# Moving the first loads into the order of use, fetching raw weight tiles ahead of their preparation, and keeping the value tiles for a whole head pair

## The chip, the cores and the metric

The kernel runs on one core of a Trainium2 chip. The core has a matrix engine (TensorE, PE in the rows; PEld is its weight load), a vector engine (VectorE, DVE), an activation engine (ScalarE, ACT), a general engine (GpSimd, POOL) and a queue engine (SyncE, SP) that here issues all transfers. Each engine runs its own list of instructions in order; they meet through semaphores. The metric is device time of one execution in microseconds (us), the median of three runs.

## The reference, cut to what matters

One layer over x of 2048 tokens by 1024 features: a normalised x is projected by one weight matrix, its columns feed three branches, and an output projection and a norm end it.

```python
h = rmsnorm(x, norm_g);  p = h @ w_in          # 1664 rwkv columns, 1544 fox, 1024 gate
# rwkv: token shift, then per head a recurrence over time
w = w0 + tanh(wl) @ w_up;  a = sigmoid(a0 + al @ a_up)
state = state*decay + sa (x) (kk*a) + v (x) k;  y = state @ r      # 8 heads of 64
# fox: causal attention with a decay from the cumulated log forget gate, 8 heads of 64
s = (q @ k.T) * scale + c_q - c_k;  o = softmax(mask(s)) @ v
y = concat(y_rwkv, y_fox) * silu(gate);  out = rmsnorm(x + y @ w_out, final_g)
```

## The kernel before, in words

Every product with `w_in` is made from halves: x and the weights are each split into a float16 high part and a float16 low part, and three matmuls (high by high, low by high, high by low) make one product. So a raw weight tile (128 columns, 512 KB of float32) has to be prepared before use: `prep_w` (L192) issues its load (L199), DVE takes its largest values (`am_`, L200, once per tile), PE turns them over the partitions (`px_`, L170 and L177), DVE works out a power of two per column group and scales the tile (L216), ACT copies the high half (L218) and POOL subtracts for the low half (L219). Raw tiles live in the three buffers of the tag `wr`; one is free again when POOL has made its low half.

**The first stage** (to about 1020 us) runs over four head pairs p and, in each, over four blocks b of 512 tokens. `load_x_block` (L138) loads four x tiles of a block, normalises and transposes them. At p = 0 each block also projects the low-rank columns (`pj_l`). Each (p, b) projects three weight tiles (`pj_r`, L254), shifts them, and runs `prep` (L471), a chain over DVE, ACT, POOL and PE that ends in the products `pb` and `pk` (L541, L544) and in stores (`d_ga`, `d_gl`, `d_ar`, `d_nk`, `d_vn`, `d_bo`). `inverse` (L574) inverts the triangular blocks of a finished pair, mostly on DVE, and `inverse_end` (L601) ends with the store `d_z` of the tile `z` (L619). Constants at L34 say at which b these happen: weights of the next pair at b = 2, inverse of the last pair at b = 1, its end at b = 2.

**Fillers.** `step(n)` draws n units from the generator `fillers` (L390): per unit one block of a fox projection (`fox_proj`, matmuls `pf`, L332) or half a gate column group (`gate_proj`). There are seven groups of three (once two) weight tiles; the weights of a group are prepared by `group_w` (L383) after the first unit of the group before. `fox_proj` also writes the value tiles `vh`, `vl` (L320 to L322, L346, L347) and stores them to `d_v`.

**Order.** The source gives the program's order; a scheduler then places each engine's instructions by its own timing model, so that the lists of all engines change when a piece of code moves. The engines follow the lists strictly: an instruction that waits holds all behind it on its engine. The later stages are attention with the rwkv chain in its gaps (about 1020 to 1460 us) and the output projection (to the end).

**Start.** Loads are issued in this order: `g_c`, four x tiles of block 0, the low-rank weight tile `wr_l`, `mu_c`, five columns of per-channel parameters (`w0_c` to `rk_c`, 2 KB each, 512 runs of one element), two of the three tiles of pair 0 (the third needs a `wr` buffer that `wr_l` holds), the forget columns `wf`, further parameter columns, `lup`, and then x blocks 1 to 3. In the rows `w_c` and `a_c` are `w0_c` and `a0_c`, `hw_c`, `ha_c`, `hka_c` and `oka_c` what DVE derives from these columns, `x`, `xt` the x tiles, `xp` their transposes, `hhi`, `hlo` the halves of x.

Of the kernel before, what the change touches and what calls it, by code (L numbers as in the profile page):

```python
# [39 lines left out]
def hymba_body(tc, x, norm_g, w_in, rw_mu, rw_w_up, rw_w0, rw_a_up, rw_a0, rw_k_k, rw_k_a, rw_r_k,  # L40
# [7 lines left out]
    with ctx:  # L48
# [32 lines left out]
        def pcol(src, n, name):  # L81
            t = ctile(name, [128, n])
            nc.sync.dma_start(t, src.rearrange("o (j p) -> p (o j)", p=128))
            return t
# [104 lines left out]
            ts(isc[:, 0:n].bitcast(I32), e, 23, ALU.logical_shift_left)  # L189
            return sc  # L190

        def prep_w(n, offs, tag, outs, iall):  # L192

            nt = len(offs)
            am = wp.tile([128, 3, KT, 2], F32, name="am_" + n, tag="am")
            wrs = []
            for i, c0 in enumerate(offs):
                wr = wp.tile([128, KT, 128], F32, name=f"wr_{n}{i}", tag="wr", bufs=3)
                nc.sync.dma_start(wr, w_in[0, :, c0:c0 + 128].rearrange("(k p) n -> p k n", p=128))  # L199
                nc.vector.tensor_reduce(am[:, i].rearrange("q k g -> q (k g)"),  # L200
                                        wr.rearrange("q k (g c) -> q (k g) c", c=64), AX.X, ALU.max,
                                        apply_absolute_value=True)
                wrs.append(wr)
# [17 lines left out]
        def load_tiles(name, offs):  # L221

            iall = wp.tile([128, 6], F32, name="ia_" + name, tag="ia", bufs=2)
            ws = [(wp.tile([128, KT, 128], F16, name=f"wh_{name}{i}", tag="wh", bufs=3),
                   wp.tile([128, KT, 128], F16, name=f"wl_{name}{i}", tag="wl", bufs=3)) for i in range(len(offs))]
            prep_w(name, offs, "r", ws, iall)
            return ws, iall

        def load_w(name, offs, extra=None):
# [4 lines left out]
            cs = [slice(128 * i, 128 * i + 128) for i in range(len(offs))]  # L234
            prep_w(name, offs, "f", [(wh[:, :, c], wl[:, :, c]) for c in cs], iall)
# [69 lines left out]
        def fox_proj(p, fw, w):  # L305
# [7 lines left out]
            nc.vector.tensor_copy(iq, isc[:, 0:4])  # L313
            i2 = F(f"i2{p}", "i2", (128, 4), bufs=2)
            nc.vector.scalar_tensor_tensor(i2, iq, 1.0 / HD, iq, ALU.mult, ALU.mult)
            for b in range(NB):
                u = f"{p}_{b}"
                t0 = b * TB
                hh, hl = hT[b]
                vh = F("vh" + u, "vh", (128, 2, 4, 66), F16)  # L320
                vl = F("vl" + u, "vl", (128, 2, 4, 64), F16)
                nc.gpsimd.memset(vh[:, :, :, 64:66], 1.0)  # L322
                qkt = [F(f"qkt{u}_{i}", f"qt{i}", (128, 2, TB), F16) for i in range(2)]
                qkn = []
# [86 lines left out]
        with c1:  # L411
# [224 lines left out]
            sml, sol = mix_scales("l", iscl, 1, mu_c[:, 12:13], omu_c[:, 12:13])  # L636

            def rw_weights(p):
                ws, isc = load_tiles(f"r{p}", [i * 512 + p * 128 for i in range(3)])
                sm, so = mix_scales(f"r{p}", isc, 3, mu_c[:, p:p + 9:4], omu_c[:, p:p + 9:4])  # L640
                return ws, sm, so

            rw = [rw_weights(0)]
# [15 lines left out]
            uh = sp.tile([128, 2, 512], F32R, name="uh")  # L659
            ul = sp.tile([128, 512], F32R, name="ul")  # L660
            up = T("lup", "rs")
            nc.sync.dma_start(up[0:64, :], rw_w_up[0])
            nc.sync.dma_start(up[64:128, :], rw_a_up[0])
            for i, (q0, q1) in enumerate(HR):
                for o0, o1 in HR:
                    nc.scalar.activation(uh[o0:o1, i], up[q0:q1], AF.Copy)
                nc.gpsimd.tensor_tensor(ul[q0:q1], up[q0:q1], uh[q0:q1, i].bitcast(F32), ALU.subtract)
            for b in range(1, NB):
                load_x_block(b, sp, ps_r)
# [488 lines left out]
```

## Time and profile before

| | us |
|---|---|
| median of three runs (1704.86, 1715.65, 1716.54) | 1715.65 |
| the profiled execution | 1709.08 |
| its span, first to last instruction | 1707.4 |
| mean granted TensorE clock, as a share of 2.4 GHz | 0.962 |

The page gives for each engine its busy time; rows of a time line give start, duration, engine, line, operation, what is written from what, and in brackets the idle time before and what ended it. Wait rows give who waited for whom, the sum, the number of waits and the longest. The profiled execution lies 6.6 us under the median.

### The profile page before, as it was taken

Reading aid. Unit: us, or ns where it says so; the run is one execution under the profiler, and the core shown is the slowest. Engines: PE = TensorE matmul, PEld = TensorE weight load, DVE = VectorE, ACT = ScalarE, POOL = GpSimd, SP = SyncE. Lnnn points to the kernel's source line nnn. Section 1 sums busy time; section 2 is a strip of 40 time slices with the busy share of each in tenths; the row PEclk is TensorE's granted clock in tenths of the full one; section 3 lists DMA queues with packets and bytes.
Section 4 is the critical chain, followed back from the end, with each engine's and each line's share of the span. In section 5 each row is a group of like instructions: output and inputs, shape, how many; then the busy total and the mean of one; then the engine's idle time right before and its main releaser. Section 6 shows DMA issues by size and latency. Waiting matters only on the chain. (4 is left out here: it accounts for less than half of the span.)

```text
span 1707.4 us, 36607 instructions
## 1 busy us (share of the span) xinstructions
PE 1575.2 (92%) x14182; PEld 974.5 (57%) x14182; DVE 1210.0 (71%) x2614; ACT 839.9 (49%) x1583; POOL 766.9 (45%) x838
## 2 busy tenths in 40 slices
PE   4899799899998999999999999899999998899998
PEld 2455355455544564445453566566666665567886
DVE  4866568975888669743844678588999997975443
ACT  5644444445433454445343247566776677564221
POOL 5754554545345543532201135455666666663000
PEclk9899899999998999999999999899999998899999
DMA  6432232233213242322234029666879633733452
GB/s 180 124 100 87 97 114 87 87 112 122 103 69 118 82 143 74 117 96 106 96 102 130 26 63 253 158 150 159 186 169 208 144 99 79 214 99 103 164 173 75
DMA packets 211983, 207.74 MB, mean 122 GB/s; under 512 B 53664, under 2 KB 173472, under 8 KB 211296
## 3 DMA queue, kind: packets, MB, share of 16 engines
q1 hardware_dynamic: 211808, 205.39, 42.1%
q8 instruction: 112, 1.84, 0.5%
q14 instruction: 63, 0.52, 0.1%
HBM read 123.34 MB, written 81.94 MB: 120 GB/s over the span
## 5 line engine op out<-in xcount | busy, mean ns | idle before, releaser
L1012 POOL TENSOR_TENSOR pl<-p,ph 128x512 f16<-128x512 f32 (+3 forms) x216 | 234.5, 1095 | 175.1 <-ACT ph L1010 70.3
L1006 ACT ACTIVATE p<-st,be 128x512 f32<-128x512 f32 (+1 forms) x320 | 193.5, 621 | 125.5 <-PE st L999 32.1
L951 DVE TENSOR_REDUCE mx<-sq 128x1 f32<-128x384 f32 (+6 forms) x320 | 184.5, 600 | 22.3 <-PE sq L947 11.6
L332 PE MATMUL pf<-fh_f,hhi 128*128 128x386 f16 x512 | 171.3, 335 | 2.1 <-DVE fl L348 1.0
L332 PE MATMUL pf<-fl_f,hhi 128*128 128x386 f16 x512 | 170.2, 332 | 1.9 <-POOL fl_f L219 1.9
L332 PE MATMUL pf<-fh_f,hlo 128*128 128x386 f16 x512 | 170.3, 333 | 0.0
L254 PE MATMUL pj_r<-hhi,wh_r 128*128 128x512 f16 x384 | 147.7, 385 | 1.3 <-ACT wh_r L218 1.2
L254 PE MATMUL pj_r<-hlo,wh_r 128*128 128x512 f16 x384 | 147.6, 384 | 0.0
L254 PE MATMUL pj_r<-hhi,wl_r 128*128 128x512 f16 x384 | 147.4, 384 | 0.0
L332 PEld LDWEIGHTS <-hhi 128*128 128x128 f16 x1024 | 100.1, 100 | 78.6 <-issue 14.6
L341 POOL TENSOR_TENSOR fr<-ft,nhalf 128x4 f32<-128x4 f32 x64 | 65.8, 1029 | 173.9 <-DVE ft L101 167.8
L1016 PE MATMUL pv<-va,ph 128*128 128x65 f16 x1088 | 133.4, 197 | 9.6 <-DVE ot L1026 7.6
L1020 PE MATMUL pv<-va,pl 128*128 128x65 f16 x1088 | 130.2, 197 | 4.6 <-POOL pl L1012 2.5
L1018 PE MATMUL pv<-vb,ph 128*128 128x64 f16 x1088 | 132.5, 195 | 0.0
L1010 ACT ACTIVATE ph<-p 128x512 f16<-128x512 f32 (+3 forms) x220 | 121.0, 561 | 13.1 <-PE pv L1020 6.8
L254 PEld LDWEIGHTS <-wh_r 128*128 128x128 f16 x768 | 74.9, 99 | 87.3 <-issue 6.5
L999 PE MATMUL st<-qb,kb 68*128 68x512 f16 (+1 forms) x320 | 114.6, 361 | 10.4 <-DMA qb<-gl 10.2
L998 PE MATMUL st<-qa,ka 128*128 128x512 f16 (+1 forms) x320 | 114.3, 360 | 6.9 <-ACT p L1006 3.9
L1016 PEld LDWEIGHTS <-ph 128*128 128x128 f16 x1088 | 102.9, 99 | 26.6 <-DVE ot L1026 9.9
L947 PE MATMUL sq<-km,qb 66*128 66x384 f16 (+6 forms) x320 | 107.0, 353 | 10.1 <-DVE mx L951 5.2
L1020 PEld LDWEIGHTS <-pl 128*128 128x128 f16 x1088 | 102.6, 99 | 22.6 <-POOL pl L1012 5.7
L1018 PEld LDWEIGHTS <-ph 128*128 128x128 f16 x1088 | 103.0, 100 | 7.7 <-issue 1.2
(378 smaller groups left out, 4068.4 us busy)
## 6 DMA issues: line engine op xcount, KB each, us to landing
d_ga<-ga SPq DMA_DIRECT2D x32, 256.0 KB
d_gl<-gl SPq DMA_DIRECT2D x32, 256.0 KB
d_nk<-nkt SPq DMA_DIRECT2D x32, 256.0 KB
d_gate<-gv SPq DMA_DIRECT2D x32, 256.0 KB
G<-d_ga SPq DMA_DIRECT2D x32, 256.0 KB
G<-d_gl SPq DMA_DIRECT2D x32, 256.0 KB
NK<-d_nk SPq DMA_DIRECT2D x16, 512.0 KB
xr<-in_x_dram SPq DMA_DIRECT2D x16, 512.0 KB
```

The costliest lines, as they stand in the source:

```text
L254: nc.tensor.matmul(ps, a[:, kt, o:o + 128], h[:, kt, :], start=n == 0, stop=n == 3 * KT - 1)
L332: nc.tensor.matmul(ps, a[:, kt, js], w[:, kt, :], start=n == 0, stop=n == 3 * KT - 1)
L947: nc.tensor.matmul(ps[:, :w], qb[0:66, i * 128:i * 128 + 128], km[0:66, ks], start=True, stop=not last)
L951: nc.vector.tensor_reduce(mx[:, i, b:b + 1], ps[:, :w], AX.X, ALU.max)
L998: nc.tensor.matmul(ps[:, c0:], ka[:, k0:k0 + 128], qa[:, q0 + c0:q0 + 512], start=True, stop=False)
L999: nc.tensor.matmul(ps[:, c0:], kb[0:68, k0:k0 + 128], qb[0:68, q0 + c0:q0 + 512], start=False, stop=not diag)
L1006: nc.scalar.activation(p32[:, c0:], ps[:, c0:], AF.Exp, bias=be[:, j:j + 1])
L1010: nc.scalar.activation(ph[:, c0:], p32[:, c0:], AF.Copy)
L1012: eng.tensor_tensor(pl[:, c0:], p32[:, c0:], ph[:, c0:], ALU.subtract)
L1016: nc.tensor.matmul(pv[:, qq, 0:65], ph[:, s_], vh[:, j, 0:65], start=j == 0 and qq == 0, stop=False, skip_group_check=True)
L1018: nc.tensor.matmul(pv[:, qq, 0:64], ph[:, s_], vl[:, j], start=False, stop=False, skip_group_check=True)
L1020: nc.tensor.matmul(pv[:, qq, 0:65], pl[:, s_], vh[:, j, 0:65], start=False, stop=fin, skip_group_check=True)
```

## The change

Nothing of what is computed changes; the number and size of the weight and x transfers are the same.

- **Start.** `wr_l` gets a buffer of its own (tag `mab`), so that the three tiles of pair 0 follow at once, then `lup` and its halves, then the parameter columns. x blocks 1 and 2 are emitted ahead of the first filler step, block 3 behind it.
- **Fetch ahead.** `fetch_w` issues raw tiles apart from `prep_w`. Weights of the next pair are fetched at b = 2 into buffers that are free then, two in the tile of the tag `z` (`wz`) and one in that of `mu` (`wm`), and prepared at b = 3. A filler group's tiles are fetched ahead of the group's predecessor and prepared after that one's second unit. `inverse` moves from b = 1 to b = 0, `inverse_end` from b = 2 to b = 1, since `z` and `mu` are theirs too.
- **Value tiles.** `vh` and `vl` are allocated and the ones written once per head pair: 4 POOL memsets of 128x8x2 in place of 16.

```diff
-P_W, P_INV, P_END = 2, 1, 2
+P_F, P_W, P_INV, P_END = 2, 3, 0, 1
...
+        def fetch_w(n, offs, tiles=None):
+            wrs = tiles or [wp.tile([128, KT, 128], F32, name=f"wr_{n}{i}", tag="wr", bufs=3) for i in range(len(offs))]
+            for wr, c0 in zip(wrs, offs):
+                nc.sync.dma_start(wr, w_in[0, :, c0:c0 + 128].rearrange("(k p) n -> p k n", p=128))
+            return wrs
...
-            for i, c0 in enumerate(offs):
-                wr = wp.tile([128, KT, 128], F32, name=f"wr_{n}{i}", tag="wr", bufs=3)
-                nc.sync.dma_start(wr, w_in[0, :, c0:c0 + 128].rearrange("(k p) n -> p k n", p=128))
+            for i, wr in enumerate(wrs):
                 nc.vector.tensor_reduce(am[:, i].rearrange("q k g -> q (k g)"),
...
+            vh = F(f"vh{p}", "vh", (128, 2, 4, 66), F16)
+            vl = F(f"vl{p}", "vl", (128, 2, 4, 64), F16)
+            nc.gpsimd.memset(vh[:, :, :, 64:66], 1.0)
             for b in range(NB):
...
-                vh = F("vh" + u, "vh", (128, 2, 4, 66), F16)
-                vl = F("vl" + u, "vl", (128, 2, 4, 64), F16)
-                nc.gpsimd.memset(vh[:, :, :, 64:66], 1.0)
...
             for i, (kind, n) in enumerate(groups):
+                more = i + 1 < len(groups)
+                if more:
+                    wrs = group_fetch(i + 1)
                 gen = fox_proj(n, fw, w) if kind == "f" else gate_proj(n, min(3, 8 - n), w)
                 next(gen)
                 yield
-                w = group_w(i + 1, fw) if i + 1 < len(groups) else None
+                next(gen)
+                yield
+                w = group_w(i + 1, wrs, fw) if more else None
                 yield from gen
...
-            whl, wll, iscl = load_w("l", [1536])
+            whl, wll, iscl = load_w("l", fetch_w("l", [1536], [sp.tile([128, KT, 128], F32, name="wr_l", tag="mab", bufs=2)]))
...
+            rw = [rw_weights(0, rw_fetch(0))]
...
+            nc.sync.dma_start(up[0:64, :], rw_w_up[0])
...
+                w0_c = pcol(rw_w0, 4, "w0_c")
...
+            load_x_block(1, sp, ps_r)
+            load_x_block(2, sp, ps_r)
             step(1)
+            load_x_block(3, sp, ps_r)
...
-                        rw.append(rw_weights(p + 1))
+                        rw.append(rw_weights(p + 1, wnext))
...
+                    if p < 3 and b == P_F:
+                        w2 = T(f"wz{p}", "z", 1, (128, 2, KT, 128))
+                        w1 = T(f"wm{p}", "mu", 1, (128, KT, 128))
+                        wnext = rw_fetch(p + 1, [w2[:, 0], w2[:, 1], w1])
```

How the lists of instructions move, at the three places that matter. First the start: DVE, from the last reduction of the low-rank tile's maxima on (`m_l`, `dg_l`, `pe_l` are that tile's scale). Before:

```order
L207 TENSOR_REDUCE mx_l<-am_l 128x2
L267 TENSOR_TENSOR wf<-wf,g_c 128x64
L657 TENSOR_TENSOR gk_c<-qg_c,kg_c 128x1
L164 TENSOR_TENSOR hlo_146<-xp_1_1_185,hhi_145 128x4x128
L269 TENSOR_REDUCE fm<-wf 128x8
L101 TENSOR_SCALAR gk_c<-gk_c 128x1
L172 TENSOR_REDUCE m_l<-px_l 2x1
L103 TENSOR_SCALAR m_l<-m_l 2x1
L101 TENSOR_SCALAR dg_l<-ident,m_l 2x2
```

The same stretch of DVE in the change:

```order
L210 TENSOR_REDUCE mx_l<-am_l 128x2
L164 TENSOR_TENSOR hlo_146<-xp_1_1_185,hhi_145 128x4x128
L172 TENSOR_REDUCE m_l<-px_l 2x1
L164 TENSOR_TENSOR hlo_146<-xp_2_0_201,hhi_145 128x4x128
L103 TENSOR_SCALAR m_l<-m_l 2x1
L101 TENSOR_SCALAR hw_c<-w_c 128x4
L101 TENSOR_SCALAR ha_c<-a_c 128x4
L101 TENSOR_SCALAR hka_c<-ka_c 128x4
L103 TENSOR_SCALAR oka_c<-ka_c 128x4
L101 TENSOR_SCALAR dg_l<-ident,m_l 2x2
```

The two readers of late columns (`wf`, `gk_c`) no longer stand ahead of the low-rank scale; the readers of `w_c` to `ka_c`, which stood earlier, now do.

Second, DVE at block 2 of pair 0, where the maxima of pair 1's weights (`am_r`) are taken (`nL_2`, `rs_2`, `nk_2`, `ga_2` are steps of `prep`). Before:

```order
L487 SCALAR_TENSOR_TENSOR nL_2_1878<-rmask,nlw_2_1873 128x512
L200 TENSOR_REDUCE am_r_1726<-wr_r_1727 128x16
L101 TENSOR_SCALAR rs_2_1881<-ss_2_1883 128x512
L200 TENSOR_REDUCE am_r_1726<-wr_r_1730 128x16
L505 SCALAR_TENSOR_TENSOR nk_2_1898<-sh_r_1830,kk_c,rs_2_1881 128x512
L103 TENSOR_SCALAR rs_2_1881<-th_2_1875,hka_c,oka_c 128x512
L200 TENSOR_REDUCE am_r_1726<-wr_r_1733 128x16
```

In the change:

```order
L101 TENSOR_SCALAR rs_2_1783<-ss_2_1785 128x512
L204 TENSOR_REDUCE am_r_2181<-wz_2131 128x16 x2
L204 TENSOR_REDUCE am_r_2181<-wm_2132 128x16
L346 TENSOR_TENSOR qk_2_0_1980<-pf_2_0_1955,fr_2_0_1986 128x256
L318 SCALAR_TENSOR_TENSOR i_2887<-iq_2885 128x4
L520 SCALAR_TENSOR_TENSOR nk_2_1800<-sh_r_1732,kk_c,rs_2_1783 128x512
```

The maxima stand behind `rs_2` instead of ahead of it, and read `wz` and `wm`, whose loads were issued in block 1.

Third, SP in block 2 of pair 1, where pair 2's weights are loaded. Before (the store `d_z` of pair 0 stands 40 rows further down, in block 3):

```order
L303 DMA d_q_67<-qkt_0_0_2896 128x512
L303 DMA d_q_68<-qkt_0_0_2896 128x512
L199 DMA wr_r_3626<-in_w_in_dram 128x8x128
L303 DMA d_k_69<-qkt_0_1_2897 128x512
L303 DMA d_k_70<-qkt_0_1_2897 128x512
L199 DMA wr_r_3629<-in_w_in_dram 128x8x128
L199 DMA wr_r_3632<-in_w_in_dram 128x8x128
```

In the change:

```order
L545 DMA d_ga<-ga_2_1_3892 128x512
L634 DMA d_z<-z_3138 128x2048
L196 DMA wz_4163<-in_w_in_dram 128x8x128 x2
L532 DMA d_bo<-rs_2_3815 128x512
L566 DMA d_ar<-ar_2_0_3856 128x256
L565 DMA d_gl<-gl_2_0_3855 128x512
L577 DMA d_nk<-nkt_2_0_3881 128x512
```

Two of the three raw tiles now stand right behind the store that reads out the buffer they go into, and five stores of `prep` stand behind them. Pair 2 has the same pattern.

## Rows read from the trace of the kernel before

**Rows 1.** The page, busy time and share of the span by engine.
```profile
PE 1575.2 (92%) x14182; PEld 974.5 (57%) x14182; DVE 1210.0 (71%) x2614; ACT 839.9 (49%) x1583; POOL 766.9 (45%) x838
```
**Rows 2.** Windows: us, busy (count) per engine, granted clock, DMA share, GB/s.
```profile
0.00:60.00 60.00, 30.58 (x117) 17.50 (x118) 35.51 (x104) 34.00 (x55) 36.65 (x49) 0.89 0.59 167
...
180.00:210.00 30.00, 18.82 (x118) 9.98 (x116) 15.81 (x35) 13.56 (x20) 18.13 (x22) 0.77 0.34 110
210.00:900.00 690.00, 658.81 (x4780) 358.89 (x4779) 486.75 (x1062) 305.16 (x562) 285.48 (x340) 0.98 0.31 102
...
1020.00:1460.00 440.00, 405.15 (x6147) 276.62 (x6146) 378.89 (x801) 298.07 (x570) 265.06 (x265) 0.95 0.70 163
```
**Rows 3.** Time line of SP's issues, start.
```profile
5.25 4.88 SPq L83 DMA_DIRECT2D w_c<-in_rw_w_dram  x1
...
33.45 0.38 SPq L199 DMA_DIRECT2D wr_r<-in_w_in_dram  x1
```
**Rows 4.** DMA view of 0 to 20 us: GB/s in 40 slices of 0.5 us.
```profile
GB/s 0 0 0 0 4 86 106 369 377 385 434 426 393 401 410 410 402 330 345 305 76 6 4 1 5 5 4 66 159 272 344 329 318 298 255 105 22 5 1 1
```
**Rows 5.** Time line of DVE, start.
```profile
13.61 0.17 DVE L101 TENSOR_SCALAR hka_c<-ka_c 128x4 f32<-128x4 f32 x1
...
19.13 0.22 DVE L267 TENSOR_TENSOR wf<-wf,g_c 128x64 f32<-128x64 f32 x1 [4.47 <-DMA wf<-in_w_in_dram]
22.33 0.16 DVE L657 TENSOR_TENSOR gk_c<-qg_c,kg_c 128x1 f32<-128x1 f32 x1 [2.97 <-DMA kg_c<-in_fox_k_g_dram]
...
23.72 0.22 DVE L101 TENSOR_SCALAR dg_l<-ident,m_l 2x2 bf16<-2x2 f32 x1
...
37.20 1.22 DVE L200 TENSOR_REDUCE am_r<-wr_r 128x16 f32<-128x1024 f32 x1 [0.87 <-DMA wr_r<-in_w_in_dram]
```
**Rows 6.** Time line of ACT, start.
```profile
23.89 0.63 ACT L666 ACTIVATE uh<-lup 64x512 fp32r<-64x512 f32 x1 [8.63 <-DMA lup<-in_rw_w_up_dram]
```
**Rows 7.** Time line of PE, start.
```profile
15.61 0.42 PE L170 MATMUL px_l<-ident,mx_l 128*2 128x128 f32 x1
...
39.67 0.27 PE L170 MATMUL px_r<-ident,mx_r 128*6 128x128 f32 x1
...
43.77 1.27 PE L161 MATMUL xp<-ident,xt 128*128 128x128 f32 x8 [3.08 <-DVE m_r L103]
...
52.38 0.61 PE L254 MATMUL pj_r<-hhi,wh_r 128*128 128x512 f16 x1 [1.19 <-ACT wh_r L218]
```
**Rows 8.** Time lines of POOL, SP, DVE and PE from 184 us.
```profile
184.01 6.09 POOL L219 TENSOR_TENSOR fl_f<-wr_f,fh_f 128x1024 f16<-128x1024 f32 x3
...
186.09 4.41 SPq L199 DMA_DIRECT2D wr_r<-in_w_in_dram  x3
...
189.81 1.22 DVE L200 TENSOR_REDUCE am_r<-wr_r 128x16 f32<-128x1024 f32 x1 [9.52 <-DMA wr_r<-in_w_in_dram]
...
192.12 1.22 DVE L200 TENSOR_REDUCE am_r<-wr_r 128x16 f32<-128x1024 f32 x1 [0.48 <-DMA wr_r<-in_w_in_dram]
...
200.48 0.48 PE L541 MATMUL pb<-ga,bk 64*64 64x128 f32 x2 [11.18 <-DVE bk L532]
```
**Rows 9.** Waits of 0 to 1020 us: waiter, awaited, sum, times, longest.
```profile
POOL vh L322 <- DMA d_v<-vh: 26.4, 10, 4.0
DVE am_g L200 <- DMA wr_g<-in_w_in_dram: 26.1, 7, 5.9
...
DVE am_f L200 <- DMA wr_f<-in_w_in_dram: 10.9, 4, 5.8
```
**Rows 10.** Time line of PE, one late weight scale of a gate group.
```profile
696.22 0.16 PE L177 MATMUL px_g<-dg_g,ones 6*128 6x6 bf16 x1 [1.78 <-DVE dg_g L101]
```
**Rows 11.** Time lines of SP and DVE: the store of the last `z`, and its buffer free.
```profile
881.96 0.32 SPq L619 DMA_DIRECT2D d_z<-z  x1
...
886.02 0.17 DVE L862 MEMSET gs<- 32x128 f16 x1 [1.94 <-DMA d_z<-z]
```
**Rows 12.** Time line of PE in the attention stage.
```profile
1075.45 0.61 PE L999 MATMUL st<-qb,kb 68*128 68x512 f16 x1 [7.50 <-DMA qb<-gl]
```

More of the change, by code (lines that the diff above doesn't have):

```diff
@@ L190, in pow2_scale, with prep_w @@
             return sc
-        def prep_w(n, offs, tag, outs, iall):
-            nt = len(offs)
+        def fetch_w(n, offs, tiles=None):
[3 more added lines that the diff above has]
+            return wrs
+        def prep_w(n, wrs, tag, outs, iall):
+            nt = len(wrs)
             am = wp.tile([128, 3, KT, 2], F32, name="am_" + n, tag="am")
-            wrs = []
-            for i, c0 in enumerate(offs):
-                wr = wp.tile([128, KT, 128], F32, name=f"wr_{n}{i}", tag="wr", bufs=3)
-                nc.sync.dma_start(wr, w_in[0, :, c0:c0 + 128].rearrange("(k p) n -> p k n", p=128))
+            for i, wr in enumerate(wrs):
                 nc.vector.tensor_reduce(am[:, i].rearrange("q k g -> q (k g)"),
@@ L202, in prep_w @@
                                         apply_absolute_value=True)
-                wrs.append(wr)
             a3 = am[:, 0:nt].rearrange("q i k g -> q (i k) g")
@@ L219, in prep_w, with load_tiles, load_w @@
                 nc.gpsimd.tensor_tensor(ol, wr, oh, ALU.subtract)
-        def load_tiles(name, offs):
+        def load_tiles(name, wrs):
             iall = wp.tile([128, 6], F32, name="ia_" + name, tag="ia", bufs=2)
             ws = [(wp.tile([128, KT, 128], F16, name=f"wh_{name}{i}", tag="wh", bufs=3),
-                   wp.tile([128, KT, 128], F16, name=f"wl_{name}{i}", tag="wl", bufs=3)) for i in range(len(offs))]
-            prep_w(name, offs, "r", ws, iall)
+                   wp.tile([128, KT, 128], F16, name=f"wl_{name}{i}", tag="wl", bufs=3)) for i in range(len(wrs))]
+            prep_w(name, wrs, "r", ws, iall)
             return ws, iall
-        def load_w(name, offs, extra=None):
+        def load_w(name, wrs, extra=None):
             wh = wp.tile([128, KT, 386], F16, name="fh_" + name, tag="fh", bufs=2)
@@ L233, in load_w @@
             iall = wp.tile([128, 6], F32, name="ja_" + name, tag="ja", bufs=2)
-            cs = [slice(128 * i, 128 * i + 128) for i in range(len(offs))]
-            prep_w(name, offs, "f", [(wh[:, :, c], wl[:, :, c]) for c in cs], iall)
+            cs = [slice(128 * i, 128 * i + 128) for i in range(len(wrs))]
+            prep_w(name, wrs, "f", [(wh[:, :, c], wl[:, :, c]) for c in cs], iall)
             if extra is not None:
@@ L381, in hymba_body, with group_fetch, group_w @@
         groups = [("f", 0), ("f", 1), ("f", 2), ("g", 0), ("g", 3), ("g", 6), ("f", 3)]
-        def group_w(i, fw):
+        def group_fetch(i):
             kind, n = groups[i]
             if kind == "f":
-                c, fs = OFF_FOX + n * 128, slice(2 * n, 2 * n + 2)
-                return load_w(f"f{n}", [c + j * 512 for j in range(3)], (fw[0][:, :, fs], fw[1][:, :, fs]))
-            return load_w(f"g{n}", [OFF_GATE + (n + j) * 128 for j in range(min(3, 8 - n))])
+                return fetch_w(f"f{n}", [OFF_FOX + n * 128 + j * 512 for j in range(3)])
+            return fetch_w(f"g{n}", [OFF_GATE + (n + j) * 128 for j in range(min(3, 8 - n))])
+        def group_w(i, wrs, fw):
+            kind, n = groups[i]
+            if kind == "f":
+                fs = slice(2 * n, 2 * n + 2)
+                return load_w(f"f{n}", wrs, (fw[0][:, :, fs], fw[1][:, :, fs]))
+            return load_w(f"g{n}", wrs)
         def fillers():
+            wrs = group_fetch(0)
             fw = forget_w()
-            w = group_w(0, fw)
+            w = group_w(0, wrs, fw)
             yield
             for i, (kind, n) in enumerate(groups):
+                more = i + 1 < len(groups)
+                if more:
+                    wrs = group_fetch(i + 1)
                 gen = fox_proj(n, fw, w) if kind == "f" else gate_proj(n, min(3, 8 - n), w)
@@ L621, in hymba_body, with rw_fetch, rw_weights @@
             load_x_block(0, sp, ps_r)
-            whl, wll, iscl = load_w("l", [1536])
+            whl, wll, iscl = load_w("l", fetch_w("l", [1536], [sp.tile([128, KT, 128], F32, name="wr_l", tag="mab", bufs=2)]))
             with nc.allow_non_contiguous_dma("small parameter columns"):
                 mu_c = pcol(rw_mu, 13, "mu_c")
+            omu_c = derived("omu_c", mu_c, -1.0, ALU.mult, 1.0, ALU.add)
+            sml, sol = mix_scales("l", iscl, 1, mu_c[:, 12:13], omu_c[:, 12:13])
+            def rw_fetch(p, tiles=None):
+                return fetch_w(f"r{p}", [i * 512 + p * 128 for i in range(3)], tiles)
+            def rw_weights(p, wrs):
+                ws, isc = load_tiles(f"r{p}", wrs)
+                sm, so = mix_scales(f"r{p}", isc, 3, mu_c[:, p:p + 9:4], omu_c[:, p:p + 9:4])
+                return ws, sm, so
+            rw = [rw_weights(0, rw_fetch(0))]
+            uh = sp.tile([128, 2, 512], F32R, name="uh")
+            ul = sp.tile([128, 512], F32R, name="ul")
+            up = T("lup", "rs")
+            nc.sync.dma_start(up[0:64, :], rw_w_up[0])
+            nc.sync.dma_start(up[64:128, :], rw_a_up[0])
+            for i, (q0, q1) in enumerate(HR):
+                for o0, o1 in HR:
+                    nc.scalar.activation(uh[o0:o1, i], up[q0:q1], AF.Copy)
+                nc.gpsimd.tensor_tensor(ul[q0:q1], up[q0:q1], uh[q0:q1, i].bitcast(F32), ALU.subtract)
+            with nc.allow_non_contiguous_dma("small parameter columns"):
                 w0_c = pcol(rw_w0, 4, "w0_c")
@@ L629, in hymba_body @@
                 rk_c = pcol(rw_r_k.rearrange("o h d -> o (h d)"), 4, "rk_c")
-            omu_c = derived("omu_c", mu_c, -1.0, ALU.mult, 1.0, ALU.add)
             hw0_c = derived("hw0_c", w0_c, 0.5, ALU.mult)
@@ L635, in hymba_body @@
             oka_c = derived("oka_c", ka_c, -0.5, ALU.mult, 1.0, ALU.add)
[L636 to L643, printed above, removed]
+            load_x_block(1, sp, ps_r)
+            load_x_block(2, sp, ps_r)
             step(1)
+            load_x_block(3, sp, ps_r)
             with nc.allow_non_contiguous_dma("small parameter columns"):
@@ L658, in hymba_body @@
             ts(gk_c, gk_c, 0.125, ALU.mult)
[L659 to L669, printed above, removed]
             mabs = []
```

## The prediction

> **What bounds the kernel now.** I read the page first, then the windows by stage, then the idle time on PE's time line with what ended it, and last the time lines of the engines named there. PE is busy for 1575.2 of 1707.4 us [rows 1], so at most 132 us can be won by filling it, and the change removes no PE work. The windows say where the gaps lie [rows 2]: 29.4 us in the first 60, 11.2 between 180 and 210, 31.2 in the 690 us after that, 34.9 in attention. The first two are dense enough to have one cause each; the rest is spread over dozens of gaps of a microsecond or two.
>
> *The start.* PE turns the low-rank tile's maxima at 15.61 [rows 7], but the scale that hangs on them, `dg_l`, is made only at 23.72 [rows 5]. DVE stood in between for two things that it does not need yet: `wf` (4.47 us) and `gk_c` (2.97 us), whose columns were still on their way. ACT stood 8.63 us for `lup` until 23.89 [rows 6]. Later the third raw tile of pair 0 is issued at 33.45, when its buffer is free [rows 3], and its maxima are taken at 37.20 after 0.87 us of waiting [rows 5]. PE gets `px_r` at 39.67, stands 3.08 us before 43.77 and starts the first `pj_r` at 52.38 [rows 7]. From 60 us on it is nearly always busy.
>
> *Around 190 us.* Read from POOL onwards [rows 8]: POOL makes low halves of a filler group from 184.01 to 190.1, each freeing a `wr` buffer; SP, which waited for these, issues pair 1's three tiles from 186.09; DVE, whose next instruction is `am_r`, stands 9.52 us until the first has landed at 189.81; behind it in DVE's list stand `rs_2`, `nk_2`, `ga_2`, which ACT, POOL and PE need; PE stands 11.18 us until 200.48. The reader should see that nobody waits for `am_r` itself; what is queued behind it costs the time.
>
> **The change, part by part.** The sum is made against the profiled execution, 1709.08 us, which is 6.57 under the median of 1715.65; I carry the difference over to the median.
>
> *Start.* DVE's list now has `dg_l` ahead of `wf` and `gk_c`, so the 4.47 and 2.97 us no longer stand in its way. What is late next are the columns: their readers stand before `dg_l`, and `w_c` to `rk_c` are now issued behind three weight tiles and `lup`, 1.75 MB more. That data runs at about 400 GB/s (369 to 434 over 3.5 to 9.5 us [rows 4]), so 4.4 us. Before, `hka_c` ran at 13.61 without waiting [rows 5]; now I put it at 18.0, and `dg_l`, two short instructions on, at 18.5: 5.2 us earlier than 23.72. `lup` is issued ahead of the columns, so ACT's 8.63 us shrink as well; that wait ended with DVE's and is no second gain. The third tile no longer waits for a buffer, 0.87 us at most on that path. I take 6. Between: at most 10, if the 3.08 us and the 0.87 go too; at least nothing, if the wait only moves, since `gk_c` now stands ahead of the end of `am_r`'s chain and its last column is issued behind two more x tiles. [...]
>
> *Pair 1's weights.* The tiles go into `wz` and `wm`, free since block 3's x tiles were transposed, and are issued in block 1; `am_r` also stands behind `rs_2` now. The 9.52 us go, and with them PE's 11.18. The granted clock of 180 to 210 us is 0.77 [rows 2], so 13.8 of these 30 us were at 1.2 GHz; 11.2 of them PE stood, and the other 2.6 cost 1.3. Full price 12.5; nothing if another late instruction stands in the same place. I take 12: in the new list three fox products of 24 matmuls each stand ahead of that `pb`, so PE has other work there.
>
> *Filler groups.* Maxima of gate and fox groups waited 26.1 and 10.9 us for their tiles [rows 9], but DVE is busy for 71% [rows 1] and PE mostly had matmuls queued; what came out on PE is a wait like the 1.78 us for `dg_g` [rows 10]. I take 1, between 0 and 4.
>
> *Value tiles.* 12 memsets of POOL go, and POOL's 26.4 us of waiting for `d_v` at them, 4.0 at most each [rows 9]. I cost this at nothing: POOL is busy 45% [rows 1]. The wait falls now on ACT's first write to `vh`, which had to wait for the memset anyway. Without that cover one `d_v` costs up to 4.0.
>
> *Added: `d_z`, then `wz`.* For pairs 2 and 3 two tiles go into the buffer that `d_z` reads out. The last `d_z` was issued at 881.96 and its buffer was free at 886.0 [rows 11]: 4.0 us. From issue to the first `am_r` a tile took 189.81 less 186.09, 3.7 us, the second 2.3 more [rows 8]. So the second tile is there 10.0 us after `inverse_end`. SP stands the first 4 of these, with `d_bo`, `d_ar`, `d_gl` and `d_nk` behind it; the buffers that these free are wanted by DVE and ACT half a block later, so this is covered; if it were not, 4 us each. Between `inverse_end` and that `am_r` PE's list has two fox products and a part of a `pj_r`, which cover most of the 10. I take 1 us each, 2 in all, between 0 and 25 (two stalls at the full 12.5 of pair 1).
>
> *`inverse` and `inverse_end` a block earlier.* DVE's list starts the inverse of a pair at the same place as before; only its end moves. No cost.
>
> *The rest.* The same instructions, in another order, also in attention. The trace does not show the new order. The nearest row is a wait of 7.50 us of PE there for a 4-KB transfer queued behind bulk loads [rows 12]; such a one may go or come: 0, between -8 and +8.
>
> Sum: -6 - 12 - 1 + 2 = -17. The profiled execution would take 1692.1, the median 1715.65 - 17 = **1698.6 us**, 1.0% less.
>
> **Rivals.** (a) *Both gains in full and more*: 10 + 12.5 + 4 - 0, and one wait like rows 12 gone, 7.5: -34, so 1682. For it: the gaps are PE's and PE is the bound. Against: 31 and 35 us of small gaps in the other windows show that something always waits next.
> (b) *The start keeps its length*, because the columns or `gk_c` are late in their new place: -12 - 1 + 2, so 1704.6. For it: SP stood 4.88 us at `w_c`, and more is ahead of it now.
> (c) *Pair 1's stall is replaced*: the filler group's weights are now prepared in the same block 2 as pair 1's, so DVE, ACT and POOL have six tiles there. If that takes the gain, -6 - 1 + 2: 1710.6.
> (d) *Slower: SP and DVE wait at `d_z` and `wz`.* If DVE meets `am_r` before `wz` has landed, in both pairs, each costs what pair 1's stall cost, 12.5: -6 - 12 - 1 + 25 = +6, so 1721.6. It decides from a delay of `inverse_end` of about 10 us against the scheduler's plan. For it: pair 1's tiles came 9.5 us late by that same plan. Against: there are only some 10 us of chain to hide and a block's matmuls beside them.
> That the change would not do what it says I exclude: the lists of instructions show the loads moved.
>
> **How the numbers follow.** Forecast 0.52, (a) 0.20, (b) 0.10, (c) 0.08, (d) 0.10. The forecast's own range is 1691 to 1707 (start 0 to 10 is half of it, attention the other). From 1682, near (a), to 1712, past (c), it holds all but the outer half of (a) and most of (d): 8 in 10. A measurement here cannot tell less than 1%, 17.2 us, from no change; that limit, 1698.5, lies at the forecast. Faster by over 1%: 0.20 of (a), half of the forecast, 0.02 of (b): 0.48. Slower by over 1%, past 1732.8: a part of (d) with stores held up too, 0.05. Within: 0.47.
>
> **What would show it.** Right, step by step: `dg_l` at about 18 to 19 us and the first `pj_r` at about 46; no wait of DVE at pair 1's `am_r` and no gap of PE over 3 us between 160 and 220; `am_g`, `am_f` out of the list of waits; waits of DVE for `wz` of 3 us or less. Wrong: PE idle in the first 60 us still near 29; a gap of 8 us or more behind `wz`; a gap of PE in attention that has grown by as much as the early ones shrank.

## The result, and the profile after

| | before | changed |
|---|---|---|
| median of 18 runs each, us | 1713.33 | 1726.62 |
| lowest and highest | 1704.86, 1722.43 | 1714.15, 1738.83 |
| profiled execution, its span | 1709.08, 1707.4 | 1717.66, 1715.8 |

The change made the kernel slower: ratio 1.0084, 95% interval 1.006 to 1.0107, or 14 us where 17 us of gain were forecast. The profiled execution of the changed kernel lies 9 us under its median, that of before 4; the profiles show 8.4 us of difference.

The page of the changed kernel, busy time by engine, and its windows by stage (columns as in [rows 2]):

```profile
PE 1570.7 (92%) x14182; PEld 972.7 (57%) x14182; DVE 1231.1 (72%) x2614; ACT 843.2 (49%) x1583; POOL 765.9 (45%) x826
```
```profile
0.00:60.00 60.00, 30.95 (x120) 17.62 (x121) 39.94 (x103) 33.06 (x53) 38.12 (x52) 0.86 0.62 175
60.00:180.00 120.00, 111.42 (x683) 62.80 (x682) 72.81 (x157) 58.32 (x112) 54.75 (x70) 0.96 0.32 102
180.00:210.00 30.00, 28.96 (x179) 15.37 (x177) 25.02 (x56) 14.72 (x24) 17.25 (x18) 1.00 0.16 53
210.00:900.00 690.00, 647.56 (x4740) 350.85 (x4738) 500.74 (x1068) 307.81 (x562) 293.12 (x340) 0.98 0.33 107
...
1020.00:1460.00 440.00, 397.68 (x6040) 273.19 (x6037) 371.06 (x782) 294.46 (x558) 260.30 (x259) 0.94 0.67 156
```

Against [rows 2]: PE idles 1.0 us where it stood 11.2 (180 to 210), so that gain is there. The first 60 us have 29.1 of idle time against 29.4: no gain. From 210 to 900 it is 42.4 against 31.2, in attention 42.3 against 34.9: losses.

The start of the changed kernel, DVE, then PE's time line (answers to [rows 5, 7]):

```profile
19.56 1.01 DVE L101 TENSOR_SCALAR hw_c<-w_c 128x4 f32<-128x4 f32 x1 [2.47 <-DMA w_c<-in_rw_w_dram]
...
20.56 0.15 DVE L101 TENSOR_SCALAR hka_c<-ka_c 128x4 f32<-128x4 f32 x1
...
20.70 0.21 DVE L101 TENSOR_SCALAR dg_l<-ident,m_l 2x2 bf16<-2x2 f32 x1
25.43 0.21 DVE L270 TENSOR_TENSOR wf<-wf,g_c 128x64 f32<-128x64 f32 x1
```
```profile
20.97 0.16 PE L177 MATMUL px_l<-dg_l,ones 2*128 2x2 bf16 x1 [2.69 <-DVE dg_l L101]
...
46.41 0.61 PE L257 MATMUL pj_r<-hhi,wh_r 128*128 128x512 f16 x1 [1.80 <-ACT wh_r L221]
...
89.73 0.66 PE L161 MATMUL xp<-ident,x 128*128 128x128 f32 x4 [2.62 <-DVE hlo L164]
95.95 0.59 PE L257 MATMUL pj_r<-hhi,wh_r 128*128 128x512 f16 x1 [5.57 <-DVE lt L459]
```

`dg_l` comes 3.0 us earlier and the first `pj_r` 6.0, and then PE stands 8.2 us at 87 to 96, where before it stood 1.9.

What the first stage ends in is read from three tiles on PE: `pZ`, the end of the last inverse; `pf`, the fox products; and `pX`, the first product of each step of the rwkv chain. The tile view gives line, count, durations in ns (least, median, most), and first and last start. Before, then changed:

```profile
L615 PE MATMUL pZ<-z,qs x512: 191/191/212, 420.7 to 880.5; 32*32 32x32 f32 x171
L332 PE MATMUL pf<-fh_f,hlo x512: 324/325/528, 90.8 to 1018.9; 128*128 128x386 f16 x171
L737 PE MATMUL pX<-SV,G x512: 222/222/370, 1032.8 to 1414.0; 128*64 128x64 f32 x171
```
```profile
L630 PE MATMUL pZ<-z,qs x512: 191/191/212, 371.9 to 858.6; 32*32 32x32 f32 x171
L335 PE MATMUL pf<-fh_f,hlo x512: 324/325/528, 104.6 to 1019.3; 128*128 128x386 f16 x171
L759 PE MATMUL pX<-SV,G x512: 222/222/367, 1033.4 to 1424.4; 128*64 128x64 f32 x171
```

The last inverse ends 21.9 us earlier, yet the last fox product comes 0.4 later. The chain starts 14 us after it in both; from its first `pX` to its last it takes 391 us in place of 381, and what follows 291 in place of 293: that is the 8.4 us. So the time is lost behind `pZ`, not where weights are fetched. An earlier `pZ` is not yet a gain: 62 gate products that stood ahead of the last `pZ` stand behind it in the change.

### The profile page after: what moved, and what is told of

It is laid out like the page before. It is cut to its first block, busy times and chain, and to the rows that moved or that the text cites. A ratio compares the mean times of both kernels' runs of the same rounds, so it can differ in the third digit from the quotient of the medians.

```text
span 1715.8 us, 36561 instructions
## 1 busy us (share of the span) xinstructions
PE 1570.7 (92%) x14182; PEld 972.7 (57%) x14182; DVE 1231.1 (72%) x2614; ACT 843.2 (49%) x1583; POOL 765.9 (45%) x826
## 5 line engine op out<-in xcount | busy, mean ns | idle before, releaser
L1028 ACT ACTIVATE p<-st,be 128x512 f32<-128x512 f32 (+1 forms) x320 | 193.0, 621 | 136.6 <-PE st L1024 42.3
L969 PE MATMUL sq<-km,qb 66*128 66x384 f16 (+6 forms) x320 | 106.5, 355 | 14.1 <-DMA km<-d_nc 7.8
L1042 PEld LDWEIGHTS <-pl 128*128 128x128 f16 x1088 | 102.7, 99 | 25.7 <-DVE pl L1034 7.2
```

What stands on the lines that cost most here:

```text
L969: nc.tensor.matmul(ps[:, :w], qb[0:66, i * 128:i * 128 + 128], km[0:66, ks], start=True, stop=not last)
L1028: nc.scalar.activation(p32[:, c0:], ps[:, c0:], AF.Exp, bias=be[:, j:j + 1])
L1042: nc.tensor.matmul(pv[:, qq, 0:65], pl[:, s_], vh[:, j, 0:65], start=False, stop=fin, skip_group_check=True)
```

## The experiments

Ratios are against before, with 95% intervals, and us are the ratio less 1, times 1712.

**The parts alone.** e1 is the start:

```diff
-            whl, wll, iscl = load_w("l", [1536])
+            whl, wll, iscl = load_w("l", fetch_w("l", [1536], [sp.tile([128, KT, 128], F32, name="wr_l", tag="mab", bufs=2)]))
...
+            load_x_block(1, sp, ps_r)
+            load_x_block(2, sp, ps_r)
             step(1)
+            load_x_block(3, sp, ps_r)
```

> Only the start of the change on the kernel before. Its order is that of before outside the first 180 us. Theory A (the start is paid back: the transposes of x blocks 1 to 3 stand later, and PE waits for them near 90 us, 2.6 + 5.6 us in the profile after, where before had 1.9): first pj_r near 46, idle time of PE in 60 to 180 us up by about 6, the whole 0 to +4 us against before. Rival B (those two waits come from another part, pair or filler weights): first pj_r near 46, no such waits, -6 us. Rival C: the 60 to 180 us cost more than the start gives and the start alone makes most of the loss: +7 us or more.

Measured 1.0042 (1.0023 to 1.0060), +7.2 us: rival C by size, with the waits of theory A (`lt` is the tile of the shifted low-rank projection). Its PE at the gap:

```profile
89.64 0.66 PE L161 MATMUL xp<-ident,x 128*128 128x128 f32 x4 [2.50 <-DVE hlo L164]
95.86 0.59 PE L257 MATMUL pj_r<-hhi,wh_r 128*128 128x512 f16 x1 [5.57 <-DVE lt L447]
96.24 0.63 PE L257 MATMUL pj_r<-hlo,wh_r 128*128 128x512 f16 x1
96.67 0.63 PE L257 MATMUL pj_r<-hhi,wl_r 128*128 128x512 f16 x1
```

The gap costs more than itself: `pj_r` follow each other at 0.43 us behind it, until 101.4, and at 0.215 before it. The granted clock is 1.00 (2.4 GHz) from 80 to 87 us and 0.50 (1.2 GHz) behind the gap; in the gap DVE is busy throughout (columns as in [rows 2]):

```profile
87.00:96.00 9.00, 0.92 (x6) 0.59 (x6) 9.00 (x11) 1.03 (x3) 7.38 (x7) 0.74 0.59 161
96.00:101.40 5.40, 5.40 (x14) 1.80 (x13) 4.58 (x6) 2.82 (x5) 5.15 (x6) 0.50 0.14 41
```

e2 is the pair weights with the earlier inverse, e3 adds the fillers, e4 is the value tiles alone:

```diff
-P_W, P_INV, P_END = 2, 1, 2
+P_F, P_W, P_INV, P_END = 2, 3, 0, 1
...
-                        rw.append(rw_weights(p + 1))
+                        rw.append(rw_weights(p + 1, wnext))
```

> Only pair weights fetched a block ahead (with the inverse a block earlier), the start, the fillers and the value tiles as before. Theory A (the loss is made by the new order of this part: the waits of PE for prep's products, ar, bk, th, carry, are 11 us more between 210 and 900 us, and 9 more in attention): pair 1's stall of 11 us gone, the whole +5 to +12 us. Rival B (the loss is the fillers' or the start's): -10 to -12 us.

> Pair weights and filler weights fetched ahead, start and value tiles as before. If the filler part makes the loss (its weights are prepared a unit later, in the same blocks as the pairs'), this is 10 us or more above the pair part alone; if it does not, within 4 us of it, and both with the loss or both without.

> Only the value tiles once per pair: the lists of all engines are those of before but for 12 memsets of POOL. Theory: 0, within 2 us, ACT's first write to vh waits for the store in POOL's stead. Rival: that wait of up to 4.0 us per unit now lies on ACT, ahead of the copies that prep needs, and costs +3 to +10 us.

e2: 1.0039 (1.0023 to 1.0056), +6.7, though PE's idle time at 180 to 210 us is gone (0.2 us). e3: 1.0021 (1.0005 to 1.0037), +3.6: the filler part costs nothing. e4: 0.9986 (0.9968 to 1.0004), nothing. So two parts lose: the start, and something in the pair part that gives back more than 11 us.

**Inside the pair part and the start.**

```diff
-P_W, P_INV, P_END = 2, 1, 2
+P_W, P_INV, P_END = 2, 0, 1
```

> The kernel before with the inverse a block earlier alone (starts at b = 0, ends at b = 1); weights, start, fillers, value tiles as before. In e2_pair PE won 11 us at pair 1's weights and lost 11 more between 210 and 900 us and about 4 in attention. Theory A (the inverse a block earlier makes that loss, since it puts DVE's inverse beside work that it held up less before): pair 1's stall stays and the whole is +8 to +15 us. Rival B (the loss is made by weights that are prepared at b = 3, or by attention's new order): within 4 us of before.

e5: 1.0022 (1.0004 to 1.0040), +3.8: below theory A, and rival B's size, at its edge. e6 fetches ahead for pair 1 alone:

```diff
-                        rw.append(rw_weights(p + 1))
+                        rw.append(rw_weights(p + 1, wnext if p == 0 else rw_fetch(p + 1)))
...
+                    if p == 0 and b == 1:
+                        w2 = T("wz0", "z", 1, (128, 2, KT, 128))
+                        w1 = T("wm0", "mu", 1, (128, KT, 128))
+                        wnext = rw_fetch(1, [w2[:, 0], w2[:, 1], w1])
```

> The kernel before with the fetch ahead for pair 1 alone (into the buffers of z and mu, issued in block 1, prepared in block 2 as before; nothing of the inverse moves, pairs 2 and 3 as before). Theory A: the stall of 11 us at pair 1 goes and nothing is given back: -8 to -12 us. Rival B (the time comes back wherever the lists are reordered, since DVE's prep chain and not PE's stall sets the pace of the first stage): no gap over 3 us at 190 us, but within 4 us of before.

e6: 0.9932 (0.9912 to 0.9953), -11.6, theory A. Its PE from 180 to 210 us, the columns as in [rows 2]:

```profile
180.00:210.00 30.00, 29.80 (x198) 16.89 (x197) 21.17 (x47) 15.39 (x28) 17.30 (x19) 1.00 0.16 58
```

e7 and e8 split the start: e7 without its x blocks (they stand behind the filler step again), e8 with the x blocks alone.

> The start as in e1 (three weight tiles and lup ahead of the parameter columns, own buffer for the low-rank tile), but x blocks 1 to 3 emitted behind the filler step and the later columns, as before. e1 lost 8.1 us of PE at 90 to 96 us, where the lists put pj_r of block 1 ahead of the first fox product and it waits for lt. Theory A (the earlier x blocks make that order): the fox product stands ahead again, no such wait, 0 to -5 us. Rival B (the order of the loads makes it): the wait stays, +5 to +9 us.

> The kernel before with x blocks 1 and 2 emitted ahead of the filler step and block 3 behind it, and nothing else: loads of weights, lup and columns as before. Theory A (the earlier x blocks make the loss of e1): PE waits 5 us or more for lt near 95 us, +4 to +9 us. Rival B: within 3 us of before.

e7: 1.0009 (0.9988 to 1.0030); e8: 1.0007 (0.9986 to 1.0029). Neither half costs or wins; both have the wait for `lt` (3.2 and 4.9 us): either half brings it. e7 goes against both its theories, e8 has rival B's size with theory A's wait.

**Next round.** e9 is the change without its start, e10 is e2 with the inverse left at 1 and 2, e11 is e1 with another buffer for `lt`, e12 is e6 with the value tiles.

```diff
-P_F, P_W, P_INV, P_END = 2, 3, 0, 1
+P_F, P_W, P_INV, P_END = 2, 3, 1, 2
```
```diff
-                lt = T(f"lt{b}", "th")
+                lt = T(f"lt{b}", "mab", 2)
```

> The whole change but its start: pair and filler weights fetched ahead and value tiles once per pair, loads at the start in the order of before. Theory A (the parts add up: start +7.2 us in e1, the other parts together +3.6 in e3 less 2.4 in e4): about +1 us against before, and the granted clock back to about 0.960 from the 0.954 of the whole change. Rival B (the parts make each other worse): +6 us or more.

> Pair weights fetched at b = 2 into the buffers of z and mu and prepared at b = 3, as in e2, but the inverse starts and ends at b = 1 and 2 as before (the fetch stands behind the store of z). e2 was +6.7 us, e6 (pair 1 alone, inverse as before) -11.6, e5 (inverse alone) +3.7. Theory A (the inverse's move, which also turns attention's lists over, makes e2's loss): -8 to -12 us. Rival B (weights prepared at b = 3 in pairs 2 and 3 make it): 0 to +7 us.

> The start as in e1, and the tile lt of the low-rank projection in a buffer of the tag mab, which is free in pair 0, in place of th's, so that it need not wait for block 0's last reader of th (bk). Theory A (that wait, 5.6 us at 95.9, with the 2.5 us ahead of it, is what the start costs): both waits gone, attention's lists unchanged, -2 to +2 us against before. Rival B (the start's cost is elsewhere): +5 us or more with no gap over 3 us near 95 us.

> Fetch ahead for pair 1 alone, as in e6, with value tiles once per pair. Sum of e6 (-11.6) and e4 (-2.4): about -14 us, 1698 to 1700. Rival: nothing beyond e6, -10 to -12.

e9: 1.0011 (0.9993 to 1.0029), theory A; within the change the start costs 12. e10: 1.0082 (1.0054 to 1.0110), +14: both theories wrong. Here rival (d) of the prediction happens in part, since `d_z` and the fetch come late: DVE waits 4.9 us for `wz` in pairs 2 and 3 together, and PE stands 3.4 and 2.1 us behind. That is a fifth of (d)'s 25 and not the 14; the rest stays open. DVE and PE of e10, pair 2:

```profile
429.90 1.22 DVE L204 TENSOR_REDUCE am_r<-wz 128x16 f32<-128x1024 f32 x1 [2.35 <-DMA wz<-in_w_in_dram]
431.61 1.22 DVE L204 TENSOR_REDUCE am_r<-wz 128x16 f32<-128x1024 f32 x1 [0.49 <-DMA wz<-in_w_in_dram]
```
```profile
433.98 0.27 PE L170 MATMUL px_r<-ident,mx_r 128*6 128x128 f32 x1 [3.38 <-DVE mx_r L210]
```

e11: 1.0073 (1.0044 to 1.0102), +12.5, rival B by size: my account of the start fell. `lt` waits no more, and the same 5.60 us stand at the next instruction, one of the x blocks' transposes:

```profile
94.95 1.09 PE L161 MATMUL xp<-ident,x 128*128 128x128 f32 x4 [5.60 <-POOL bk L536]
```

e12: 0.9934 (0.9911 to 0.9957), -11.3: e6 and no more.

**The last pair.** In p = 3 no weights are fetched, so nothing forces the earlier inverse there. e13 is the change with it as before in that pair alone, e14 the same without the start, e15 start, pair 1 and value tiles, e16 the change with late x blocks.

```diff
-                    if p and b == P_INV:
+                    if p and b == P_INV + (p == 3):
...
-                    if p and b == P_END:
+                    if p and b == P_END + (p == 3):
```

> The whole change, but in the last pair (p = 3), where no weights are fetched, the inverse of pair 2 starts and ends at b = 1 and 2 as before. The lists are those of the change up to pair 3, and those of before, or nearly, in attention. Theory A (attention's lists, turned over by the inverse of that pair, cost about 8 us: idle time of PE behind 1020 us 51 to 56 us in the five kernels with the earlier inverse, 43 to 50 in the nine others): 6 to 10 us below the change, +0.2 to +0.5% against before. Rival B (attention loses only because its work comes there late or at a lower clock): within 3 us of the change, +0.7 to +0.9%.

> The same without the start: pair and filler weights fetched ahead, value tiles once per pair, the last pair's inverse as before. e9 (the same with the earlier inverse) was +1.9 us. Theory A: -4 to -8 us against before. Rival B: 0 to +4.

> Start, pair 1's weights ahead and value tiles; inverse, pairs 2 and 3 and fillers as before. Lists of all engines behind some 500 us are those of before. Theory A (parts add up: +7.2 - 11.6 - 2.4, and 0 for the lists behind): -5 to -9 us. Rival B (the start costs more beside other parts, as within the change, 12.5): -2 to +1.

> The whole change with x blocks 1 to 3 emitted behind the filler step as before. The start without its x blocks (e7) was +1.6 us, with them (e1) +7.2. Theory A (they add up): 5 to 6 us below the change, +0.5% against before. Rival B: within 2 us of the change.

e13: 0.9922 (0.9898 to 0.9946), 13.4 us faster than before and 28 than the change, by two conditions; theory A had the direction and a third of the size. With the end alone moved back, the lists of all five engines come out the same as e13's, so the end counts and not the begin. e14: 0.9913 (0.9882 to 0.9945), -14.9, past theory A and the lowest ratio here; but its interval overlaps those of e13, e12 and e6, so e6's few lines give most of it. e9 and e14 differ in the last pair's inverse alone: 17 us. e15: 0.9984 (0.9960 to 1.0007), -2.7, between its theories. e16: 1.0139 (1.0110 to 1.0167), +24, against both theories: its last `pf` stands within 1 us of the change's (1018.5 us), and 11 us more are lost behind it; why stays open. e13 in the tile view:

```profile
L630 PE MATMUL pZ<-z,qs x512: 190/192/213, 371.3 to 871.2; 32*32 32x32 f32 x171
L335 PE MATMUL pf<-fh_f,hlo x512: 324/326/529, 104.0 to 1009.8; 128*128 128x386 f16 x171
L759 PE MATMUL pX<-SV,G x512: 221/222/367, 1023.7 to 1404.7; 128*64 128x64 f32 x171
```

Its last inverse ends 12.6 us later than the change's, its last fox product 9.5 us earlier. What lies between is in PE's list: from the last `pZ` to the last `pf` before has 20 `st`, 71 `sq` and 30 `pv` of attention's first heads (`st`, `sq` score products, `pv` products with the values), e13 the same, the change 38, 85 and 108. Gate products stand there too, 223, 228 and 285; but all 768 of them stand ahead of the last `pf` in every kernel, so attention's 110 are what comes on top.

e17 makes that one move on the kernel before, an earlier inverse in the last pair and nothing else:

```diff
-                    if p and b == P_INV:
+                    if p and b == P_INV - (p == 3):
...
-                    if p and b == P_END:
+                    if p and b == P_END - (p == 3):
```

> The kernel before with one thing moved: in the last pair the inverse of pair 2 starts and ends a block earlier. The lists then have 54 st, 97 sq and 204 pv between the last pZ and the last fox product pf, in place of 20, 71 and 30. Theory A (attention's work ahead of the last fox products delays the chain, which starts 14 us after them): the last pZ 8 us or more earlier, the last pf no earlier than in before, chain and what is behind it 3 to 12 us longer: +4 to +12 us. Rival B (this only hurts where weights are fetched ahead): within 3 us of before.

1.0117 (1.0089 to 1.0144), +20 us: theory A in direction, at twice its size.

```profile
L615 PE MATMUL pZ<-z,qs x512: 191/191/212, 424.0 to 880.2; 32*32 32x32 f32 x171
L332 PE MATMUL pf<-fh_f,hlo x512: 324/326/544, 91.0 to 1044.5; 128*128 128x386 f16 x171
L737 PE MATMUL pX<-SV,G x512: 221/222/370, 1058.5 to 1444.7; 128*64 128x64 f32 x171
```

Same last `pZ` as before, last `pf` 25.6 us later, chain 25.7 later, span 1735.1 in place of 1707.4. Theory A had the last `pZ` 8 us earlier and the loss in the chain; neither came, the loss is ahead of the chain. With the end alone moved, the lists come out the same as e17's, and with the begin alone, the same as before's.

The windows cut at the last `pf`, columns as in [rows 2]: before, changed, e13, e17.

```profile
0.00:1019.20 1019.20, 937.81 (x6391) 515.20 (x6392) 688.59 (x1588) 448.57 (x825) 431.23 (x512) 0.96 0.31 101
1019.20:1707.40 688.20, 637.34 (x7794) 459.29 (x7792) 521.41 (x1027) 391.38 (x759) 335.64 (x327) 0.96 0.59 152
```
```profile
0.00:1019.60 1019.60, 937.38 (x6501) 514.82 (x6502) 717.56 (x1604) 456.64 (x837) 433.80 (x504) 0.97 0.31 101
1019.60:1715.80 696.20, 633.29 (x7684) 457.87 (x7681) 513.53 (x1011) 386.57 (x746) 332.11 (x322) 0.95 0.58 150
```
```profile
0.00:1010.10 1010.10, 929.51 (x6391) 508.90 (x6392) 708.40 (x1588) 450.48 (x825) 430.23 (x500) 0.97 0.32 102
1010.10:1695.40 685.30, 635.20 (x7794) 458.28 (x7792) 516.70 (x1027) 390.61 (x759) 335.85 (x327) 0.96 0.59 153
```
```profile
0.00:1044.80 1044.80, 956.39 (x6625) 528.13 (x6626) 706.39 (x1619) 461.99 (x849) 441.22 (x520) 0.96 0.31 99
1044.80:1735.10 690.30, 629.28 (x7560) 455.26 (x7557) 509.93 (x996) 377.11 (x735) 328.92 (x318) 0.95 0.59 151
```

In e17, 234 matmuls more stand ahead of the last `pf` than before. PE is busy 18.6 us longer there and idles 7.0 more; behind it PE is busy only 8.1 us less and idles 10.2 more. In the change, against e13, it is 110 matmuls: 7.9 busy and 1.6 idle more ahead, 1.9 busy less and 12.8 idle more behind.

What holds the chain shows in SP's list: its first load, `G`. Waits of SP from 990 to 1070 us and the issue, before, then e17:

```profile
SPq L715 <- PE sq L950: 14.1, 1, 14.1
1019.11 0.66 SPq L715 DMA_DIRECT2D G<-d_ga  x1
```
```profile
SPq L715 <- PE sq L947: 17.4, 1, 17.4
1044.67 0.65 SPq L715 DMA_DIRECT2D G<-d_ga  x1
```

SP stands there for PE and issues 0.2 us after the start of the last `pf` in both. In the source `chain_all` opens the chain's pool right behind `hctx.close()`, which gives up the pools of the halves of x and of the fox weights on the same side, so its loads wait for the last readers of these.

Nine of the nineteen profiles, us (last `pZ`; from it to the last `pf`; from that to the end of the span):

| | last pZ | to pf | to the end |
|---|---|---|---|
| before | 880.5 | 138.4 | 688.5 |
| e1 start | 888.7 | 138.6 | 691.7 |
| e6 pair 1 | 874.1 | 138.1 | 689.9 |
| e14 | 864.6 | 138.7 | 686.7 |
| e13 | 871.2 | 138.6 | 685.6 |
| e17 | 880.2 | 164.3 | 690.6 |
| e5 inverse | 875.2 | 150.3 | 691.0 |
| e2 pair | 855.8 | 163.7 | 694.8 |
| changed | 858.6 | 160.7 | 696.5 |

The twelve kernels that end the last pair's inverse where before does have 136.6 to 139.0 in the second column, the seven others 150.3 to 164.3. The third column is 685.6 to 698 in all but e3 (700.8) and e16 (707.7): it does not shrink when attention's work is done ahead of the chain. PE idles 50 to 55 us behind the last `pf` in the twelve, 58 to 70 in the seven.

## Why the prediction was wrong

**The step that failed** is the one on the inverse: "DVE's list starts the inverse of a pair at the same place as before; only its end moves. No cost." The end's place in the last pair cost 20 us by itself (e17), 28 within the change (e13) and 17 within the change without its start (e14 against e9). I priced the stores and DVE's work of the step and did not ask what its new place lets go first. With the end a block earlier in the program, the scheduler's lists put attention's first heads ahead of the last fox group, and the rwkv chain starts 14 us after the last `pf` (13.8 to 14.1 us in all profiles but e5, 16.2). The page's share of busy time does not show it (92% before and changed), but windows cut at the last `pf` do: attention's work comes on top ahead of the chain, and behind it PE idles where that work had filled the chain's gaps. That the chain waits for the fox group as such is read from SP's wait, the source and the constant distance; the wait row names `sq`, which PE ran at that time, and no run parted the buffers.

Two things stay open. Of the 20 us between the profiles of the change and of e13 9.5 are there at the last `pf`, and 10.9 come behind it, spread over many waits of PE; the one that grew most, `pY` for DVE's `SV`, has 4.5 us. And e5, with the earlier end in all pairs, cost only 3.8: it has 104 matmuls more ahead of the last `pf`, which comes 6.6 us later. So the price hangs on the lists that come out and not on the place alone. The term "the rest", 0 between -8 and +8 for attention's lists, was the same blind spot.

**Start**, forecast -6, measured +7.2 alone (e1), 12 within the change (e9), 1.5 between e14 and e13, whose intervals overlap. The first `pj_r` came at 46.41, as forecast; `dg_l` at 20.70, not 18.5: `hw_c` waited for `w_c` until 19.56 and then took 1.01 us. (The rate in the sum, 369 to 434 GB/s, holds for 3.5 to 8.5 us; the two slices to 9.5 have 330 and 345 [rows 4].) That a mark comes 6 us earlier was taken for 6 us. Up to the first `pj_r` PE idled 26.6 us where it had idled 29.3, so 2.8 of the 6 were idle time, and the rest is work that now stands behind the mark; behind it, to 60 us, PE idles 2.5, where before it idled 0.1. So the prediction's own sign of being wrong came, 29.1 us of idle time in the first 60. Then PE met the next late work, 8 us at 87 to 96, and the lower clock after that. What is late there is DVE, by the rows: busy 13.53 of the 13.60 us from the first `pj_r` to 60, and all 9.0 from 87 to 96 in e1, 7.4 before. `lt`'s buffer is excluded (e11), either half of the start brings the wait (e7, e8); no run relieved DVE, so that it makes the loss is read and not shown. Rival (b), that the start keeps its length, came true by size, but not through the columns: the first `pj_r` came when it was forecast.

`w_c` was there 4.9 us after its issue at 14.70. The Trainium skill, "SBUF — State Buffer", section "The DMA setup-cost knee", gives about 2 us plus bytes over 436 GB/s for a transfer, by which a 2-KB column by itself would take an estimated 2 us. The trace has more, with three tiles and `lup` issued ahead; no run tells that queue from the column's 512 runs of one element.

**Pair 1's stall**, forecast -12: -11.6 (e6). Right in place, mechanism and size.

**Filler groups**, -1: e3 less e2 is -3.1, within the bounds, with intervals that overlap. `am_g`'s waits went from 26.1 to 2.6 us, `am_f`'s from 10.9 to 6.3; in the change:

```profile
DVE am_f L204 <- DMA wr_f<-in_w_in_dram: 6.3, 2, 4.2
DVE am_g L204 <- DMA wr_g<-in_w_in_dram: 2.6, 1, 2.6
```

**Value tiles**, 0: -2.4 with an interval over 0.

**`d_z`, then `wz`**, +2: DVE does not wait for `wz` in the changed kernel (2.6 us for `wm`), so 0; rival (d)'s waits come, smaller than priced, with the later end of e10. That the earlier inverse is what the earlier pairs need and what the last must not have is read from e10 against e14, which differ in fillers and value tiles too.

Of the 31 us between -17 and +14 the inverse is 28 and the start 7 (-6 forecast, +1.5 in e13 against e14); the other terms take 4 back. That -17 stands near e13's -13.4 is in part luck: the start's 6 us are not in it.

## What to carry to other kernels

Where a long serial chain sets the end, find what it starts behind, and count in the lists what stands ahead of that; work that moves there from the chain's gaps is paid ahead of the chain and leaves the gaps empty, and a busy share of the whole does not show it. A mark that comes earlier is a gain only if the engine's idle time shrinks with it. When a change frees a resource in a loop, move only the iterations that need it.

## What the hardware showed that was not expected

In e1 DVE's smallest instructions, beside POOL's `wl_r`, took as long as one of these. DVE, then POOL:

```profile
51.38 0.14 DVE L103 TENSOR_SCALAR xs<-xs 128x1 f32<-128x1 f32 x1
51.45 2.09 DVE L103 TENSOR_SCALAR sc_f<-pe_f 128x8 int32<-128x8 int32 x1
53.57 2.05 DVE L101 TENSOR_SCALAR sc_f<-sc_f 128x8 int32<-128x8 int32 x1
55.53 0.16 DVE L101 TENSOR_SCALAR pe_f<-pe_f 128x8 int32<-128x8 int32 x1
```
```profile
51.37 4.21 POOL L222 TENSOR_TENSOR wl_r<-wr_r,wh_r 128x1024 f16<-128x1024 f32 x2
55.55 0.59 POOL L155 TENSOR_TENSOR xr<-xs,nhalf 128x1 f32<-128x1 f32 x1
```

Two of 8 elements a partition fill the 4.21 us of POOL's two, and the next takes 0.16. It is no single case: of e1's 279 TENSOR_SCALARs of at most 16 elements a partition (median 0.17 us) 33 took over 0.6 us, and every one of the 33 ended 0.02 to 0.03 us after a POOL instruction did. DVE was busy 39.3 us in the first 60 of e1, 35.5 in before; five such instructions take 7.0 us of the one, two take 3.3 of the other, which is nearly the difference. The Trainium skill, "Trainium Architecture — The Big Picture", section "What this means for kernel authors", has the port pair of DVE and GpSimd as an exclusive lock and not a split of bandwidth; these rows agree, but no run here took POOL's instruction away.
